# A hybrid attention and Fourier block: half of the gate products placed behind the softmax maxima, context rows spread out, and banks of its own for one product

## The chip, the cores and the metric

The kernel runs on one core of one Trainium2 chip. The metric is the device time of one execution in microseconds (us). Besides the plain runs there is one profiled execution; its trace names every instruction, its engine, its start and its length. "Span" is the time from the first to the last instruction in it. The engines are TensorE (PE in the profile, with its weight loads as PEld), VectorE (DVE), ScalarE (ACT), GpSimd (POOL) and SyncE (SP, which here only issues DMAs).

## The reference

One layer (`DEPTH = 1`) on 512 latent tokens of width 2048 and 256 context tokens, all in float32. What matters of it:

```python
shift, scale, gate = jnp.split(silu_c @ w_ada[l] + b_ada[l], 3, axis=-1)
shift_c, scale_c, gate_c = jnp.split(silu_cc @ w_ada[l] + b_ada[l], 3, axis=-1)
h = _modulate(_rmsnorm(xs, norm_g[l]), shift[:, None], scale[:, None])
hc = _modulate(_rmsnorm(cs, norm_g[l]), shift_c, scale_c)
pc_kv = hc @ w_l[:, OFF_K:OFF_ZA]              # keys and values of the context
p = h @ w_l                                    # 9216 columns: q, k, v, z_a, u_b, z_b, g_a, g_b
attn = _attention(q, jnp.concatenate([k, kc], axis=1), jnp.concatenate([v, vc], axis=1))
# _merge:
y_a = (attn * jax.nn.silu(z_a)) @ w_pa
y_b = (_fourier_mix(u_b) * jax.nn.silu(z_b)) @ w_pb
y = (g_a * y_a + g_b * y_b) @ w_o              # g_a, g_b are sigmoids of columns of p
new_xs = xs + gate[:, None] * y
return _rmsnorm(new_xs, final_g)
```

There are 12 query heads of 128 on 4 key heads; each query sees 768 keys. The vector `gate` (2048 values) is needed only at the very end, as a factor of `y`.

## The kernel before, in words

**Matrix products.** Every float32 operand is split into a high and a low part (`split_from`: ACT writes the high part, line 175, DVE subtracts it for the low part, line 176), and each product is three matmuls (`mm3`, lines 324 to 326). Large products are done as a seven-product scheme of the Strassen-Winograd kind: a `Group` works through seven products named P1, Q5, P2, Q6, P7, Q3 and Q4 on half-sized operands, and DVE combines their sums. One product has four weight pieces of 128 x 1024; a piece is 12 matmuls.

**Stages.** First a start stage (norms, modulation, the Fourier branch). Then eight projection groups `g = 0..7`: three of kind "qz" (queries and z_a), two "gate" (3 and 4, for g_a), one "kv" (5, which also works on the context), two more "gate" (6 and 7, for g_b). Then the attention: 12 heads of four query tiles are `NSTEP = 48` steps. In step i TensorE makes the scores, DVE their maximum (line 1262), ACT the exponentials (line 1264), the step before is transposed and split, and every second step the values are multiplied; `fill` puts pieces of the Fourier branch's projection (`filler`, its result taken over by DVE in line 1229) between them. Last come two branch groups (10 and 11, the attention's projection) and two output groups (8 and 9). In a branch group the seven products come in the order P1, P2, Q5, P7, Q6, Q3, Q4, in fixed banks of PSUM: "a" at bank 0, "c" at 2, "b" at 4.

**Weight stream.** `todo` lists every piece to be loaded in the order of use; `load_more` asks for pieces (SP's queue, line 211) as long as raw buffers are free and fewer than eight pieces are ahead. There are four raw buffers in `wp`; `raw0` and `raw1` in `rp` and two in `gvp` are in the list `raw_pools` for some of the time. A stage-0 product's pieces go to four buffers R instead, to which further weights are added by accumulating DMAs from POOL's queue (line 279) or by DVE (line 258); P7's pieces are differences from them (line 264).

**Gate vector.** `gate` is worked out by DVE: 32 pieces of `w_gate`, each multiplied with half a row of silu(c) (`crow[0]` for pieces 0 to 15, `crow[1]` for 16 to 31) and summed along it, in one instruction with an accumulator (`use_gate`, line 1098). `GATE_AT` says after which piece of which product in the groups the first 26 are done; the other six are asked for in attention steps 5, 10, ..., 30 and used three steps later. `load_row` brings half a row to `raw0`'s place; `silu_of_row` (lines 1088 and 1089) turns it with a tanh on ACT and a product on DVE. For the second half that is called at group 6's Q5, with a tile of `gvp` as its scratch; `gvp` lies where `qr` lay.

**Context rows.** The 256 context tokens' normalized, modulated forms are made in groups 3 and 4. `context_norm` (lines 1044 to 1047) and `context_spread` make the row of inverse norms; they stand in the list `jobs`, from which one entry is taken after each weight piece (`None` entries only count). `context_piece` says behind which piece four row blocks are worked on by `context_row` (lines 1062 to 1076), which builds seven forms in the shared buffer `qr` and stores them to `cf_d`; the kv group loads them back. `qr` is also the buffer in which rotated queries and keys are stored from (`qz_d`, `k_d`).

**Order.** The program's order is not the engines' order: the framework orders each engine's instructions by a plan of its own, with the program's order as rank. `tc.issue_after(x)` puts instructions behind x on x's engine. `use_gate` uses it with the last split.

Of the kernel before, what the change touches and what calls it, by code (L numbers as in the profile page):

```python
# [25 lines left out]
NKV = 4  # L26
# [46 lines left out]
def context_piece(g, name, pc):  # L73

    n = 28 * (g - NQZ) + 4 * ONE_GROUP.index(name) + pc
    if n % 2 == 0 and 0 <= n < 8:
        return "cn", n // 2
    if n % 6 == 0 and 18 <= n < 42:
        return "cr", n // 6 - 3

# [3 lines left out]
           + [(5, "P1", 1), (5, "Q5", 1), (5, "P2", 1), (5, "Q6", 1), (5, "P7", 1), (5, "P7", 3), (5, "Q3", 1),  # L84
              (5, "Q3", 3), (5, "Q4", 0)] + [(6, n, 1) for n in ("P2", "Q6", "P7", "Q3", "Q4")]
           + [(7, n, 1) for n in ("P1", "Q5", "P2", "Q6", "P7")])
GATE_AT = {p: q for q, p in enumerate(GATE_AT)}
NGATE = len(GATE_AT)

CHUNKS = (0, 2, 1, 3)  # L90
# [28 lines left out]
def block_kernel(ctx, tc, xT, ctx_rows, ctx_toks, x, c_row, w_ss, w_gate, vecs, qkg, rope, dft_c, dft_s,  # L119
# [178 lines left out]
    def get_aside(key):  # L298

        while not any(e.key == key for e in ahead):  # L300
            assert start_load(), key
        e = next(e for e in ahead if e.key == key)
        ahead.remove(e)
        return e.raws[0][1]

# [120 lines left out]
    for i in range(2):  # L426
        stream(("b", i), flat(b_d[i]), 1024, 2, dst=lambda: tiles("b"))
    for n, j in enumerate(CHUNKS):
        for pc in BRANCH_B:
            stream(("pab", j, pc), w_pab[j, pc], 1024, 2)  # L430
        if n + 1 < NKV:
            stream_keys(n + 1)

# [362 lines left out]
    class Group:  # L796
# [16 lines left out]
        def steps(self, name):  # L813

            form, which = next((f, c) for n, f, _, c in PRODUCTS if n == name)
            start = which not in self.acc
            if start:
# [8 lines left out]
            for pc in range(self.pieces):  # L826
# [20 lines left out]
                if q is not None:  # L847
                    use_gate(q, get(("gate", q)))
            sub = lambda o, x, y: nc.vector.tensor_tensor(o, x, y, op=ALU.subtract)
# [10 lines left out]
            elif name == "Q6":  # L860
# [3 lines left out]
                if self.g >= BRANCH_A:  # L864
                    sub(self.V, self.V, self.acc["c"])
                    self.done(1, 1, self.V, self.V)
            elif name == "P7" and self.g >= BRANCH_A:
# [5 lines left out]
            elif name == "P7":  # L873
                sub(self.V, self.V, a)
                self.done(1, 1, self.V, self.V)
            elif name == "Q3":
                if not self.last:
                    sub(self.X, a, self.X)
                self.done(0, 1, a if self.last else self.X, self.X)
            elif name == "Q4" and self.g == BRANCH_A + 1:  # L880
                self.done(1, 0, a, self.Y)
            elif name == "Q4":
                for t in ((0,), (1,)) if (self.g, name, 3) in APART else ((0, 1),):
                    t = slice(t[0], t[-1] + 1)
                    sub(self.Y[:, t, :], a[:, t, :], self.Y[:, t, :])
                self.done(1, 0, self.Y, self.Y)
# [203 lines left out]

    def ask_gate(q):
        todo.insert(0, Piece(("gate", q), [w_gate[q]], 1024, 1, "raw"))
        todo[0].aside = True

    def use_gate(q, w):

        with tc.issue_after(last_split[-1][1].ins):
            nc.vector.scalar_tensor_tensor(w, w, 0.5, crow[q // KK], op0=ALU.mult, op1=ALU.mult,
# [31 lines left out]
    for g, kind in enumerate(KINDS):  # L1130
        if g == 3:
            jobs += [lambda: None] * 10 + [context_norm, lambda: None, lambda: None, context_spread]
        elif g == KV:
# [10 lines left out]
        for name in ONE_GROUP:  # L1144
# [3 lines left out]
            elif (g, name) == (1, "Q5"):  # L1148
                silu_of_row(0, flat(new_ev()))
            elif (g, name) == (KV + 1, "Q5"):  # L1150
                silu_of_row(1, gvp.tile([P, 1024], F32, tag="raw", bufs=2, name=uid("e")))
# [15 lines left out]
            elif (g, name) == (KV + 1, "Q6"):  # L1167
                raw_pools += [(rp, 1, "raw1", 1), (gvp, 2, "raw", 2)]
            elif (g, name) == (LAST, "P7"):
# [78 lines left out]
    bheld = {}  # L1248
    NSTEP = 4 * NH

    def scores(i):
# [9 lines left out]
        mx = stats[:, 4 * (i % 4) : 4 * (i % 4) + 4]  # L1261
        nc.vector.tensor_reduce(mx[:, 0:1], sc[:, :NKEY], axis=AX.X, op=ALU.max, negate=True)
        probs[i] = take((NKEY,))
# [149 lines left out]
    for i in range(NSTEP + 3):  # L1413
# [367 lines left out]
```

## Time and profile before

| | |
|---|---|
| runs | 1345.84, 1342.2 and 1351.04 us; median 1345.84 |
| profiled execution | 1343.44 us, its span 1341.6 us |
| TensorE busy | 1290.6 us, 96% of the span, mean granted clock 0.992 |
| DVE busy | 995.6 us, 74% |
| ACT busy | 682.2 us, 51% |
| POOL busy | 180.6 us, 13% |
| DMA | 318.54 MB, mean 237 GB/s |

How to read it: "x" behind a time is a count. A group of instructions is named by line, engine, operation and tile (out<-in, without buffer numbers). In the timeline a bracket at the end of a row holds how long the engine sat idle before that instruction and what ended the wait. A table of waits has the engine and line that waited, what for, the total in us, the times and the longest. In a table of stretches the clock column is the granted TensorE clock, 1.00 being full. Some matmul records can be missing from a trace.

### The profile page before, as it was taken

Reading aid. Unit: us, or ns where it says so; the run is one execution under the profiler, and the core shown is the slowest. Engines: PE = TensorE matmul, PEld = TensorE weight load, DVE = VectorE, ACT = ScalarE, POOL = GpSimd, SP = SyncE. Lnnn points to the kernel's source line nnn. Section 1 sums busy time; section 2 is a strip of 40 time slices with the busy share of each in tenths; the row PEclk is TensorE's granted clock in tenths of the full one; section 3 lists DMA queues with packets and bytes.
Section 4 is the critical chain, followed back from the end, with each engine's and each line's share of the span. In section 5 each row is a group of like instructions: output and inputs, shape, how many; then the busy total and the mean of one; then the engine's idle time right before and its main releaser. Section 6 shows DMA issues by size and latency. Waiting matters only on the chain.

```text
span 1341.6 us, 17565 instructions
## 1 busy us (share of the span) xinstructions
PE 1290.6 (96%) x6522; PEld 1052.7 (78%) x6522; DVE 995.6 (74%) x1295; ACT 682.2 (51%) x1079; POOL 180.6 (13%) x244
## 2 busy tenths in 40 slices
PE   6999999999998989999998999899999999999997
PEld 3677888888887878887886878788888778778885
DVE  5666899889777868648676847687778767788676
ACT  5222655546455444443344534566577545465544
POOL 0110011111101001011021011112100212121210
PEclk9999999999999999999998999999999999999999
DMA  9898588888887979777877888767840889898985
GB/s 384 340 374 309 203 219 223 241 227 246 223 311 193 317 229 272 262 203 188 280 201 225 315 226 259 263 194 221 219 153 19 217 250 229 232 201 223 219 214 172
DMA packets 103718, 318.54 MB, mean 237 GB/s; under 512 B 9808, under 2 KB 33104, under 8 KB 99280
## 3 DMA queue, kind: packets, MB, share of 16 engines
q0 software_dynamic: 30288, 123.75, 39.2%
q1 hardware_dynamic: 48720, 163.65, 34.1%
q10 hardware_dynamic: 24624, 30.02, 6.4%
q8 instruction: 51, 0.84, 0.2%
q14 instruction: 35, 0.29, 0.1%
HBM read 283.30 MB, written 34.09 MB: 237 GB/s over the span
## 4 chain that ended last, share of the span: by engine, by line
PE 75%; DMA 10%; DVE 8%; ACT 3%; issue 2%; POOL 0%; SPq 0%; ACTq 0%; DVEq 0%; POOLq 0%
PE banks L324 10%; PE banks L325 10%; PE banks L326 10%; PE x L325 6%; PE x L326 6%; PE x L324 6%; PE y L325 5%; PE y L324 5%; PE y L326 5%; DVE wlo L176 3%; PE banks L1280 2%; PE pd L523 2%; DMA wr<-in_w_g 2%; PE pb L324 2%; DMA R<-in_w_g 2%
## 5 line engine op out<-in xcount | busy, mean ns | idle before, releaser
L175 ACT ACTIVATE whi<-R 128x1024 fp32r<-128x1024 f32 x138 | 145.0, 1057 | 143.1 <-PE banks L326 57.7
L176 DVE TENSOR_TENSOR wlo<-R,whi 128x1024 fp32r<-128x1024 f32 x138 | 167.5, 1220 | 51.8 <-ACT whi L175 51.2
L175 ACT ACTIVATE whi<-wr 128x1024 fp32r<-128x1024 f32 (+1 forms) x123 | 128.6, 1050 | 128.9 <-PE banks L326 35.0
L176 DVE TENSOR_TENSOR wlo<-wr,whi 128x1024 fp32r<-128x1024 f32 (+1 forms) x123 | 148.4, 1211 | 60.4 <-ACT whi L175 60.2
L324 PE MATMUL banks<-whi,s 128*128 128x512 f32 x396 | 156.7, 396 | 8.9 <-DVE R L1229 3.4
L325 PE MATMUL banks<-wlo,s 128*128 128x512 f32 x396 | 155.2, 392 | 2.0 <-DVE wlo L176 2.0
L326 PE MATMUL banks<-whi,s 128*128 128x512 f32 x396 | 155.2, 392 | 0.0
L325 PE MATMUL x<-wlo,s 128*128 128x512 f32 x352 | 138.0, 392 | 6.6 <-DVE wlo L176 6.6
L324 PE MATMUL x<-whi,s 128*128 128x512 f32 x352 | 137.7, 391 | 0.0
L326 PE MATMUL x<-whi,s 128*128 128x512 f32 x352 | 137.7, 391 | 0.0
L324 PE MATMUL y<-whi,s 128*128 128x512 f32 x316 | 123.4, 391 | 0.8 <-DVE cxe L999 0.8
L325 PE MATMUL y<-wlo,s 128*128 128x512 f32 x316 | 123.3, 390 | 0.0
L326 PE MATMUL y<-whi,s 128*128 128x512 f32 x316 | 123.0, 390 | 0.0
L279 POOL DMA_DIRECT2D R<-in_w_g x64 | 55.9, 874 | 451.5 <-DVE wlo L176 246.4
L175 ACT ACTIVATE s<-wr 128x512 fp32r<-128x512 f32 (+2 forms) x93 | 59.9, 675 | 73.9 <-DMA wr<-in_w_g 21.3
L324 PEld LDWEIGHTS banks<-whi,s 128*128 128x128 f32 x396 | 74.4, 188 | 25.4 <-ACT whi L175 6.0
L176 DVE TENSOR_TENSOR s<-wr,s 128x512 fp32r<-128x512 f32 (+2 forms) x93 | 66.5, 747 | 30.8 <-ACT s L175 30.5
L325 PEld LDWEIGHTS banks<-wlo,s 128*128 128x128 f32 x396 | 74.4, 188 | 16.8 <-DVE wlo L176 2.8
L326 PEld LDWEIGHTS banks<-whi,s 128*128 128x128 f32 x396 | 74.4, 188 | 15.5
L325 PEld LDWEIGHTS x<-wlo,s 128*128 128x128 f32 x352 | 66.4, 189 | 21.2 <-DVE wlo L176 7.5
L324 PEld LDWEIGHTS x<-whi,s 128*128 128x128 f32 x352 | 66.5, 189 | 13.8
L326 PEld LDWEIGHTS x<-whi,s 128*128 128x128 f32 x352 | 66.5, 189 | 13.8
(292 smaller groups left out, 2840.5 us busy)
## 6 DMA issues: line engine op xcount, KB each, us to landing
wr<-in_w_g SPq DMA_DIRECT2D x128, 512.0 KB, 5.2
R<-in_w_g POOLq DMA_DIRECT2D x64, 512.0 KB, 7.1
wa<-in_w_ss POOLq DMA_DIRECT2D x26, 1024.0 KB, 8.1
R<-in_w_g SPq DMA_DIRECT2D x32, 512.0 KB, 6.1
wr<-in_w_gate SPq DMA_DIRECT2D x32, 512.0 KB, 5.3
wr<-in_w_o SPq DMA_DIRECT2D x24, 512.0 KB, 6.8
R<-in_w_o POOLq DMA_DIRECT2D x24, 512.0 KB, 8.0
wr<-in_w_pab SPq DMA_DIRECT2D x20, 512.0 KB, 5.8
```

The source lines that it names most:

```text
L175: first = nc.scalar.activation(hi, src, ACT.Copy)
L176: return first, nc.vector.tensor_tensor(lo, src, hi.bitcast(F32), op=ALU.subtract)
L279: nc.gpsimd.dma_start(chain[e.pc], e.nxt, accum_op=ALU.add)
L324: nc.tensor.matmul(o, ah, bh, start=start, stop=False, skip_group_check=cont)
L325: nc.tensor.matmul(o, ah, bl, start=False, stop=False, skip_group_check=cont)
L326: nc.tensor.matmul(o, al, bh, start=False, stop=stop, skip_group_check=cont)
L523: last = nc.tensor.matmul(acc[32 * j : 32 * j + 32, :256], c2[:, 8 * h + k, :], w[:, k, :], start=n < 4, stop=n >= KK - 4)
L1280: nc.tensor.transpose(tp[:, k * P : (k + 1) * P], p[:, k * P : (k + 1) * P], ident)
```

## The change

It moves work and changes banks; no matmul is added or taken out.

- The four context row blocks go from every sixth weight piece (18, 24, 30, 36, counted from the start of group 3) to every eighth (18, 26, 34, 42). `context_norm` and `context_spread` come two entries later in `jobs`.
- `GATE_AT` keeps the 16 gate pieces of the first half (its last one moves by one weight piece). The second 16 are all used in the attention, at steps 6, 8, 11, 13, ..., 41, 43, and are now part of the stream, between the weights of the filler and the keys. They are issued behind the maximum of their step (`maxima[0]`), not behind the last split. After such a piece is taken, `load_more` is called.
- `silu_of_row(1)` is called at group 6's Q3 instead of Q5, and the two raw buffers of `gvp` join the list at group 6's Q4 instead of Q6.
- In the branch groups Q3 gets banks "d", which are those of "a", and starts a sum of its own there; it was added on top of Q6's sum in "b". DVE keeps Q6's difference in V and adds Q3's sum to it.
- The weight sums that POOL's queue prepares in the attention start at step 10 instead of 8.

```diff
-    if n % 6 == 0 and 18 <= n < 42:
-        return "cr", n // 6 - 3
+    if n % 8 == 2 and 18 <= n < 50:
+        return "cr", n // 8 - 2
...
-              (5, "Q3", 3), (5, "Q4", 0)] + [(6, n, 1) for n in ("P2", "Q6", "P7", "Q3", "Q4")]
-           + [(7, n, 1) for n in ("P1", "Q5", "P2", "Q6", "P7")])
+              (5, "Q3", 3), (5, "Q4", 1)])
...
+GATE_STEPS = [n // 2 + 6 for n in range(0, 78, 5)]
...
         ahead.remove(e)
+        load_more()
         return e.raws[0][1]
...
+    q = NGATE
     for n, j in enumerate(CHUNKS):
         for pc in BRANCH_B:
             stream(("pab", j, pc), w_pab[j, pc], 1024, 2)
-        if n + 1 < NKV:
-            stream_keys(n + 1)
+        for keys in (False, True):
+            while q < 2 * KK and (GATE_STEPS[q - NGATE] < 12 * n + 9 or keys and n + 1 == NKV):
+                stream(("gate", q), w_gate[q], 1024, 1, "raw")
+                todo[-1].aside = True
+                q += 1
+            if not keys and n + 1 < NKV:
+                stream_keys(n + 1)
...
+            if name == "Q3" and self.g >= BRANCH_A:
+                which = "d"
...
-                    use_gate(q, get(("gate", q)))
+                    use_gate(q, get(("gate", q)), last_split[-1][1])
...
                 if self.g >= BRANCH_A:
-                    sub(self.V, self.V, self.acc["c"])
-                    self.done(1, 1, self.V, self.V)
+                    sub(self.X, self.V, self.acc["c"])
+                    self.done(1, 1, self.X, self.X)
...
+            elif name == "Q3" and self.g >= BRANCH_A:
+                nc.vector.tensor_tensor(self.V, self.V, a, op=ALU.add)
+                self.done(0, 1, self.V, self.V)
...
-    def use_gate(q, w):
-
-        with tc.issue_after(last_split[-1][1].ins):
+    def use_gate(q, w, line):
+
+        with tc.issue_after(line.ins):
...
-            jobs += [lambda: None] * 10 + [context_norm, lambda: None, lambda: None, context_spread]
+            jobs += [lambda: None] * 12 + [context_norm, lambda: None, lambda: None, context_spread]
...
-            elif (g, name) == (KV + 1, "Q5"):
+            elif (g, name) == (KV + 1, "Q3"):
                 silu_of_row(1, gvp.tile([P, 1024], F32, tag="raw", bufs=2, name=uid("e")))
...
             elif (g, name) == (KV + 1, "Q6"):
-                raw_pools += [(rp, 1, "raw1", 1), (gvp, 2, "raw", 2)]
+                raw_pools.append((rp, 1, "raw1", 1))
+            elif (g, name) == (KV + 1, "Q4"):
+                raw_pools.append((gvp, 2, "raw", 2))
...
-        nc.vector.tensor_reduce(mx[:, 0:1], sc[:, :NKEY], axis=AX.X, op=ALU.max, negate=True)
+        maxima[0] = nc.vector.tensor_reduce(mx[:, 0:1], sc[:, :NKEY], axis=AX.X, op=ALU.max, negate=True)
...
-        return Group(BRANCH_A + n, bf, lambda: take((2, 512)), lambda *a: branch_done(n, *a), {"a": 0, "b": 4, "c": 2}, pieces=3)
+        return Group(BRANCH_A + n, bf, lambda: take((2, 512)), lambda *a: branch_done(n, *a), {"a": 0, "b": 4, "c": 2, "d": 0}, pieces=3)
...
-        if 8 <= i < 26:
-            n, step = divmod(i - 8, 3)
+        if 10 <= i < 28:
+            n, step = divmod(i - 10, 3)
...
-        if 5 <= i < 35 and i % 5 in (0, 3):
-            n, last = NGATE + (i - 5) // 5, i % 5 == 3
-            if not last:
-                ask_gate(n)
-            else:
-                use_gate(n, get_aside(("gate", n)))
-                if n == 2 * KK - 1:
-                    raw_pools.append((rp, 1, "raw0", 1))
+        if i in GATE_STEPS:
+            n = NGATE + GATE_STEPS.index(i)
+            use_gate(n, get_aside(("gate", n)), maxima[0])
+            if n == 2 * KK - 1:
+                raw_pools.append((rp, 1, "raw0", 1))
```

More of the change, by code (lines that the diff above doesn't have):

```diff
@@ L77, in context_piece @@
         return "cn", n // 2
-    if n % 6 == 0 and 18 <= n < 42:
-        return "cr", n // 6 - 3
+    if n % 8 == 2 and 18 <= n < 50:
+        return "cr", n // 8 - 2
 GATE_AT = ([(g, n, 1) for g in (1, 2) for n in ("P2", "Q6", "Q3")] + [(3, "Q5", 1)]
            + [(5, "P1", 1), (5, "Q5", 1), (5, "P2", 1), (5, "Q6", 1), (5, "P7", 1), (5, "P7", 3), (5, "Q3", 1),
-              (5, "Q3", 3), (5, "Q4", 0)] + [(6, n, 1) for n in ("P2", "Q6", "P7", "Q3", "Q4")]
-           + [(7, n, 1) for n in ("P1", "Q5", "P2", "Q6", "P7")])
+              (5, "Q3", 3), (5, "Q4", 1)])
 GATE_AT = {p: q for q, p in enumerate(GATE_AT)}
 NGATE = len(GATE_AT)
+GATE_STEPS = [n // 2 + 6 for n in range(0, 78, 5)]
+assert len(GATE_STEPS) == 2 * KK - NGATE
 CHUNKS = (0, 2, 1, 3)
@@ L1089, in silu_of_row @@
         nc.vector.scalar_tensor_tensor(row, e, 1.0, row, op0=ALU.add, op1=ALU.mult)
-    def ask_gate(q):
-        todo.insert(0, Piece(("gate", q), [w_gate[q]], 1024, 1, "raw"))
-        todo[0].aside = True
-    def use_gate(q, w):
-        with tc.issue_after(last_split[-1][1].ins):
+    def use_gate(q, w, line):
+        with tc.issue_after(line.ins):
             nc.vector.scalar_tensor_tensor(w, w, 0.5, crow[q // KK], op0=ALU.mult, op1=ALU.mult,
@@ L1249, in block_kernel @@
     NSTEP = 4 * NH
+    maxima = [None]
     def scores(i):
```

## The prediction

> **What bounds the kernel now.** I read the page's first part, then the busy time in stretches of 20 us, then what TensorE waited for, and last the instructions around each stretch in which TensorE fell short.
>
> ```profile
> span 1341.6 us, 17565 instructions
> PE 1290.6 (96%) x6522; PEld 1052.7 (78%) x6522; DVE 995.6 (74%) x1295; ACT 682.2 (51%) x1079; POOL 180.6 (13%) x244
> ```
>
> TensorE is the bound, busy for 1290.6 of 1341.6 us. A change that removes no matmul can give back what TensorE stands idle, and what it loses to a low clock after that, and no more. Where that is:
>
> ```profile
> 400.00:420.00 20.00, 20.00 (x90) 16.57 (x89) 17.67 (x22) 12.56 (x31) 6.99 (x7) 1.00 0.88 200
> 420.00:440.00 20.00, 16.54 (x73) 13.12 (x72) 15.20 (x19) 8.50 (x10) 3.46 (x4) 1.00 0.68 198
> 480.00:500.00 20.00, 17.97 (x80) 14.55 (x78) 13.74 (x23) 9.28 (x14) 2.57 (x3) 1.00 0.81 230
> 500.00:520.00 20.00, 17.64 (x71) 14.43 (x72) 15.61 (x26) 9.71 (x15) 1.73 (x2) 0.91 0.87 287
> 700.00:720.00 20.00, 14.98 (x53) 11.56 (x52) 10.30 (x14) 7.45 (x12) 0.12 (x1) 0.83 0.71 224
> 780.00:800.00 20.00, 16.85 (x67) 13.46 (x66) 11.65 (x13) 7.31 (x10) 1.69 (x2) 0.91 0.73 218
> 840.00:860.00 20.00, 15.09 (x68) 12.19 (x67) 11.22 (x16) 9.50 (x14) 1.96 (x3) 0.91 0.90 327
> ```
>
> The columns are stretch, length, busy time (and count) of PE, weight loads, DVE, ACT and POOL, granted clock, DMA share, GB/s. An undisturbed stretch of the projections holds 90 matmuls (400 to 420), 0.222 us each. Counting short of 90 gives what each stretch lost, clock included: 17 at 420, so **3.8 us**; 10 and 19 from 480 to 520, so **6.4**; 37 at 700, so **8.2**; 23 at 780, so **5.1**. The stretch at 840 holds other shapes; it is priced below. TensorE waited there for:
>
> ```profile
> PE x L325 <- DVE wlo L176: 6.6, 2, 3.5
> PE y L325 <- DVE s L176: 4.4, 1, 4.4
> PE x L324 <- ACT s L175: 4.2, 1, 4.2
> PE banks L324 <- DVE R L1229: 3.4, 1, 3.4
> PE banks L324 <- DVE s L849: 2.8, 2, 1.4
> PE banks L324 <- DVE ptl L176: 1.3, 1, 1.3
> ```
>
> All are waits for a split or an eviction by DVE or ACT. Both average well below full load, so the question is what those engines stood behind. In order of time:
>
> ```profile
> 398.43 0.15 DVE L1044 TENSOR_TENSOR small<-small 128x2 f32<-128x2 f32 x1
> 424.80 0.28 DVE L1047 TENSOR_SCALAR qr<-ident,small 128x128 f32<-128x128 f32 x1 [6.95 <-DMA qz_d<-qr]
> 476.25 0.48 DVE L1062 SCALAR_TENSOR_TENSOR qr<-wr,gain,qr 128x256 f32<-128x256 f32 x1 [5.74 <-DMA cf_d<-qr]
> 501.22 0.48 DVE L1062 SCALAR_TENSOR_TENSOR qr<-wr,gain,qr 128x256 f32<-128x256 f32 x1 [7.48 <-DMA cf_d<-qr]
> 708.98 1.06 ACT L1088 ACTIVATE e<-crow 128x1024 f32<-128x1024 f32 x1 [8.96 <-DMA k_d<-qr]
> 786.54 1.23 DVE L264 TENSOR_TENSOR wr<-R,wr 128x1024 f32<-128x1024 f32 x1 [11.12 <-DMA R<-in_w_g]
> 850.75 1.23 DVE L1098 SCALAR_TENSOR_TENSOR wr<-wr,crow 128x1024 f32<-128x1024 f32 x1 [4.79 <-DMA wr<-in_w_gate]
> 851.91 0.95 DVE L1262 TENSOR_REDUCE gain<-banks 128x1 f32<-128x768 f32 x1
> 944.42 1.23 DVE L1098 SCALAR_TENSOR_TENSOR wr<-wr,crow 128x1024 f32<-128x1024 f32 x1 [1.76 <-DMA wr<-in_w_gate]
> ```
>
> Every gap has the same form: an instruction that nobody needs yet stands at the head of DVE or ACT, waits there for a DMA, and the splits that TensorE needs stand behind it. The rows also show that the program's order isn't the engine's order. The gate product written for attention step 8 runs at 850.75, ahead of the first maximum (851.91). L1044 begins the job context_norm, which the program calls after the third weight piece (of four) of group 3's second product, and runs at 398.43; that product's first matmul is here:
>
> ```profile
> 408.82 0.39 PE L324 MATMUL y<-whi,s 128*128 128x512 f32 x1
> ```
>
> Its third piece ends 36 matmuls later, at about 417. What is not pinned goes forward until its data are there, in the plan's reckoning of time, and the plan reckons some DMAs shorter than they are.
>
> **The change, part by part.** The sum is made against the profiled execution, 1343.44 us (span 1341.6); the median of the three runs is 2.4 us above it.
>
> *Context rows from 6 to 8 pieces apart.* The rows share one buffer, qr, and each row must wait until its predecessor's cf_d store has read it.
>
> ```profile
> 484.11 0.33 SPq L211 DMA_DIRECT2D wr<-in_ctx_rows  x1
> 490.76 0.33 ACTq L1076 DMA_DIRECT2D cf_d<-qr  x1
> ```
>
> The store issued at 490.76 releases the last row's first instruction at 501.22, and DVE stands for 7.48 us. The last row moves from piece 36 to 42 after the start of group 3. Among those six pieces four (P2's) need a raw buffer, so its load, now at 484.11, comes behind four weight loads, after about 500; the row can't stand at DVE's head before its load. Nothing then waits at 494 to 501: **-6.4 us**. The third row moves by four pieces, two of them with a load; it may still meet the wait at 476.25, which stops no matmul now (460 to 480 has no entry in TensorE's waits). Bounds: 0 if another row stands there, 6.4 if none. I take 6.4. The later last store holds the ACT queue's table load behind it some microseconds later than now; ACT stood there without cost before, I take 0 against at most the 6.4 that this place has shown.
>
> *context_norm two jobs later.* L1047 waits 6.95 us for qr. Two pieces are 5.4 us, so if the job were pinned, the wait would shrink to 1.5 and the 3.8 us would go. But the job isn't pinned; L1044 ran some 18 us ahead of its place. Bounds 0 and 3.8; the nearest row is L1044's, so **0**.
>
> *Tanh of the second half-row at Q3 instead of Q5 of group 6.* Its target lies where qr lay, and it stands at ACT's head until the k_d store has landed, 8.96 us.
>
> ```profile
> 709.95 1.14 ACT L175 ACTIVATE s<-wr 128x512 fp32r<-128x512 f32 x2
> 715.36 0.33 SPq L211 DMA_DIRECT2D wr<-in_w_gate  x1
> ```
>
> The split of P2's fourth piece (709.95) is the one TensorE waited for. With the tanh four products later in the program, the splits of P2 and Q6 rank ahead of it, and its buffer is free by 709 in any case. Also, no gate load takes a raw buffer here any more (such as the one at 715.36), so P2's fourth load goes one place earlier. If the tanh is moved forward again, it meets the same 8.96 us: bounds 0 and 8.2. I take **-8.2**, since several splits that are ready now outrank it. The two extra raw buffers come three products later; groups 3 and 4 run at 90 matmuls per stretch with no more buffers than remain, so 0.
>
> *Ten gate products out of groups 6 and 7 and into the attention, each behind its step's maximum.*
>
> ```profile
> L1098 DVE SCALAR_TENSOR_TENSOR wr<-wr,crow x32: 1205/1217/1226, 272.4 to 948.2; 128x1024 f32<-128x1024 f32 x32
> L1098 DVE DVE_READ_ACCUMULATOR wr<-wr,crow x32: 77/82/85, 273.5 to 949.3; 128x1 f32 x32
> wr<-in_w_gate SPq DMA_DIRECT2D x32, 512.0 KB, 5.3
> 843.17 0.33 SPq L211 DMA_DIRECT2D wr<-in_w_gate  x1
> 854.00:858.00 4.00, 4.00 (x19) 3.38 (x18) 1.25 (x4) 2.04 (x5) 0.55 (x1) 0.57 0.71 206
> 880.00:900.00 20.00, 20.00 (x140) 18.08 (x139) 17.36 (x29) 14.82 (x30) 3.32 (x6) 1.00 0.73 251
> 1020.00:1040.00 20.00, 20.00 (x142) 18.41 (x141) 18.91 (x30) 15.35 (x31) 0.87 (x1) 1.00 0.09 24
> ```
>
> One costs DVE 1.22 + 0.08 = 1.30 us; ten are 13 us, and ten loads of 0.5 MB go with them on SP's queue. In the attention, 880 to 900 holds two of them with TensorE at 20.00 of 20, and 1020 to 1040 has DVE at 18.91 of 20, TensorE still full. So 1.30 us every 2.5 steps (about 10 us) is hidden by the next transposes and filler matmuls. If that cover were gone, all ten cost 13. I charge one, **+1.3**, because the last (step 43) stands just ahead of the full stretch at 1020.
>
> What they give: a gate pinned behind its maximum can't stand ahead of step 0. The wait of 4.79 at 850.75 goes, and with it TensorE's 3.44 us idle and the 4 us at a clock of 0.57 behind it, 4 x 0.43 = 1.7: **-5.2**. The pair at 944 goes too, with the 1.29 on ptl: **-1.3**. This holds only if the loads are early. Following the program's requests through the five raw buffers, today's first gate finds no free buffer when it is asked for (843.17, landing 850.7); in the new order every gate is asked for at least two steps before its use, about 8 us against a median 5.3 to landing.
>
> The Trainium skill (TensorE: Matmul & The Clock Gate, the clock table) says that the clock halves after an idle window of about 3.4 us that runs freely; 854 to 858 at 0.57 agrees, while 420 to 440 at 1.00 after 3.46 us idle shows the free phase. By that rule alone, the idle at 850 would be worth 3.4 or 5.1; my sum uses the row.
>
> *Sixth product's own banks.* In the branch groups Q3 gets banks that P1 and P2 have left, so it needn't wait until DVE has read Q6's sum: L849, twice 1.4. The DVE work is the same count, three subtractions, then one addition for one subtraction. But behind the second place TensorE waits again:
>
> ```profile
> 1166.12 0.50 PE L325 MATMUL banks<-wlo,s 128*128 128x512 f32 x1 [1.28 <-DVE wlo L176]
> ```
>
> That split hangs on a weight load, not on TensorE, so coming 1.4 us earlier there only lengthens this wait. Bounds 1.4 and 2.8; I take **-1.4**.
>
> *The rest.* The weight sums two steps later keep their DMAs and are needed only after the attention; the last gate of the first half one piece later delays the row's load by some 4 us, before an ACT that is 40 us away: 0. The 5.1 at 780 (L264 behind R's accumulating DMA) isn't touched on purpose. Two gates less ahead of it and less DMA traffic could shorten it; bounds 0 and 5.1, the wait of 11.12 is far longer than 2 x 1.30, so **0**.
>
> Sum: -6.4 - 8.2 - 5.2 - 1.3 - 1.4 + 1.3 = -21.2; 1343.4 - 21.2 = **1322 us**.
>
> **Rivals.**
> *The plan goes by readiness, not by place.* The moved tanh and rows go forward again and meet the same stores. Only what is pinned or structural stays: -5.2 - 1.3 - 1.4 + 1.3 = -6.6, so 1337 us. For it: L1044's 18 us. Against: the last row's later load.
> *Everything goes.* L1047's 3.8, the 5.1 at 780 and the second 1.4 go as well, and the 1.3 is hidden: 1322.2 - 3.8 - 5.1 - 1.4 - 1.3 = 1311 us.
> *Slower: pinned gates whose loads are late.* A gate now stands right behind the maximum, ahead of the splits of the probabilities and the filler's eviction, and can't be put off. Each late load then costs what 850.75 cost, 5.2 us. With n late ones among sixteen: 1322 + 5.2 n (the two of today are already taken out); from n = 5 on it is slower than 1343.4, and with eight it is 1364. For it: five raw buffers shared with keys, values and filler weights, and loads of gates have been late twice among six. Against: the requests are earlier. The Trainium skill (TensorE: Matmul & The Clock Gate, the table of specifications) calls VectorE's queue strictly first in, first out; the row at 850.75, with the maximum behind it, agrees, and that rule is what makes this rival dear.
>
> **How the numbers follow.** Forecast 0.56, readiness 0.17, everything 0.14, late loads 0.13. What a measurement can tell apart from no change is about 1% (13 us); the three runs lie 9 us apart. The forecast's own spread is a term of 6 to 8 us up or down, so 0.51 of its 0.56 falls beyond 1%; with "everything" that is 0.65 faster. Readiness (-0.5%) and the rest of the forecast with two or three late loads make 0.24 the same, and late loads from five on 0.11 slower. The range goes from 1309, under "everything", to 1343, which takes in readiness and up to four late loads.
>
> **What would show it.** Right: no waits of DVE on cf_d near 500 and of ACT on k_d near 709, 90 matmuls in every stretch there; gates in the attention at distances of about 10 us, none with a wait on in_w_gate; no wait on L849 in the branch groups. Wrong: L1062 or L1088 again behind their stores; gates waiting for loads with a clock below 0.7 after them; a new wait on raw buffers in group 6; TensorE idle in the attention behind ptl or L1229 with no DMA involved.

## The result

The changed kernel takes 1327.74 us (median; 1325.23 to 1329.0), beside 1346.37 us for the kernel before in runs taken with it. The ratio is 0.9858, with an interval of 0.9822 to 0.9895: 1.4% faster, and 6 us above the 1322 that was forecast. Some 3 of these 6 are the base: the forecast was counted from 1343.44, and the kernel before came out at 1346.37. The gain is 18.6 us for 21.2 forecast. The profiled execution took 1329.0 us, with a span of 1327.0.

All lines of the file have moved. The conversions of the split, 175 and 176, are now 176 and 177; the diagonal product of `context_norm` is 1060, `context_row` 1075, the tanh 1101, the gate product 1107, the difference behind R 265, DVE's take-over of sums 859, the matmuls of a product 326 to 328, the exponentials 1276, the transposes of the attention 1292 and of the branch groups 1406 (before 1394).

The page's first lines, then the busy time in stretches (columns as before):

```profile
span 1327.0 us, 17532 instructions
PE 1290.2 (97%) x6522; PEld 1053.7 (79%) x6522; DVE 994.9 (75%) x1295; ACT 683.9 (52%) x1079; POOL 180.8 (14%) x244
...
420.00:440.00 20.00, 16.41 (x60) 12.94 (x59) 13.77 (x17) 8.51 (x12) 3.13 (x4) 0.83 0.68 193
480.00:500.00 20.00, 20.00 (x90) 16.57 (x89) 19.47 (x30) 9.98 (x16) 3.46 (x4) 1.00 0.65 168
500.00:520.00 20.00, 20.00 (x90) 16.57 (x89) 10.79 (x20) 9.70 (x14) 0.00 (x0) 1.00 0.93 313
520.00:540.00 20.00, 19.13 (x84) 15.48 (x84) 17.56 (x20) 8.49 (x11) 3.45 (x4) 1.00 0.94 246
540.00:560.00 20.00, 18.80 (x84) 15.12 (x83) 12.73 (x13) 11.29 (x13) 0.00 (x0) 1.00 0.92 312
700.00:720.00 20.00, 16.81 (x62) 12.97 (x61) 9.37 (x11) 8.29 (x11) 0.86 (x1) 0.83 0.62 199
780.00:800.00 20.00, 20.00 (x90) 16.57 (x89) 10.87 (x13) 9.45 (x14) 3.47 (x4) 1.00 0.92 240
900.00:920.00 20.00, 16.29 (x96) 14.18 (x96) 12.30 (x21) 10.31 (x20) 3.94 (x6) 0.83 0.81 232
```

TensorE's busy time is what it was (1290.2 after 1290.6), so all that came off is idle time. Counted against 90 matmuls as before: 480 to 520 is full (it lost 6.4 us), 780 is full (it lost 5.1). But 420 is 30 short, 6.7 us after 3.8; 700 is 28 short, 6.2 after 8.2; 520 to 560, which held 90 and 90 before, is 12 short, **2.7 us lost anew**; and 900, which held 135, holds 96.

Three rows of each trace cut the span into parts: the first matmul behind the projections, and the first and last transposes of the branch groups. First the kernel before, then after:

```profile
844.98 0.47 PE L324 MATMUL banks<-whi,s 128*128 128x512 f32 x1 [1.47 <-DVE ev L849]
1082.65 1.03 PE L1394 MATMUL banks<-ident,s 128*128 128x128 f32 x8
1188.61 1.03 PE L1394 MATMUL banks<-ident,s 128*128 128x128 f32 x8
```

```profile
837.85 0.47 PE L326 MATMUL banks<-whi,s 128*128 128x512 f32 x1 [1.47 <-DVE ev L859]
1072.91 1.04 PE L1406 MATMUL banks<-ident,s 128*128 128x128 f32 x8
1173.95 1.04 PE L1406 MATMUL banks<-ident,s 128*128 128x128 f32 x8
```

The projections are 7.1 us shorter (forecast 14.6), the attention 2.6 (237.67 to 235.06; forecast 5.2), the branch groups 4.9 (105.96 to 101.04; forecast 1.4), and the rest is equal (152.99 and 153.05). That is 14.6 us of span in all. This profiled execution is the longest of the four, and that of the kernel before was 2.9 us below its median, so this sum is smaller than the difference of the medians (18.6).

What stood at the head of DVE and ACT in the places that still lose time, and in those that no longer do:

```profile
426.02 0.28 DVE L1060 TENSOR_SCALAR qr<-ident,small 128x128 f32<-128x128 f32 x1 [6.82 <-DMA qz_d<-qr]
509.44 0.88 DVE L1075 SCALAR_TENSOR_TENSOR qr<-wr,gain,qr 128x256 f32<-128x256 f32 x2 [6.08 <-DMA cf_d<-qr]
524.73 1.29 DVE L934 SCALAR_TENSOR_TENSOR qr<-qr 128x512 f32<-128x512 f32 x2 [1.31 <-DMA qr<-in_qkg]
543.51 1.15 ACT L176 ACTIVATE s<-wr 128x512 fp32r<-128x512 f32 x2 [4.47 <-DMA wr<-cf_d]
709.27 1.06 ACT L1101 ACTIVATE e<-crow 128x1024 f32<-128x1024 f32 x1 [9.72 <-DMA k_d<-qr]
769.32 1.22 DVE L265 TENSOR_TENSOR wr<-R,wr 128x1024 f32<-128x1024 f32 x1 [1.88 <-DMA R<-in_w_g]
```

The last context row still waits 6.08 us behind its store, but no matmul needs DVE just then (480 to 520 is full). What follows it is late instead: the rotation table (L934) stands ahead of a low part at 525, and the conversion at 543 waits for the last `cf_d` to be read back. The diagonal product and the tanh are where they were, to 1.3 us, though the program calls the one two jobs and the other four products later. In place of the one wait of 11.12 us on R at 786 there are three short ones, the longest 1.88. No gate product in the attention waits for its load any more. One weight of the filler does:

```profile
893.76 0.33 SPq L212 DMA_DIRECT2D wr<-in_w_pab  x1
901.97 1.06 ACT L176 ACTIVATE whi<-wr 128x1024 fp32r<-128x1024 f32 x1 [3.62 <-DMA wr<-in_w_pab]
906.29 0.69 PE L1292 MATMUL banks<-ident,s 128*128 128x128 f32 x2 [3.70 <-ACT s L1276]
```

Its load went out at 893.76, when the gate product at 892.50 gave its raw buffer back. ACT stood before its conversion; the low part on DVE waited for that conversion, the next maxima stood behind the low part, the exponentials waited for the maxima, and TensorE was idle for 3.70 us.

### The profile page after: what moved, and what is told of

It reads as the page before. It is cut to its first block, busy times and chain, and to the rows that moved or that the text cites. A ratio compares the mean times of both kernels' runs of the same rounds, so it can differ in the third digit from the quotient of the medians.

```text
span 1327.0 us, 17532 instructions
## 1 busy us (share of the span) xinstructions
PE 1290.2 (97%) x6522; PEld 1053.7 (79%) x6522; DVE 994.9 (75%) x1295; ACT 683.9 (52%) x1079; POOL 180.8 (14%) x244
## 4 chain that ended last, share of the span: by engine, by line
PE 69%; DMA 15%; DVE 9%; ACT 4%; issue 3%; POOL 0%; ACTq 0%; SPq 0%; DVEq 0%; POOLq 0%
PE banks L326 9%; PE banks L327 9%; PE banks L328 9%; PE x L327 6%; PE x L328 6%; PE x L326 6%; PE y L327 4%; PE y L326 4%; PE y L328 4%; DMA s<-in_w_pab 3%; DVE wlo L177 3%; DMA wr<-in_w_g 2%; PE pd L531 2%; DMA cf_d<-qr 2%; DVE s L177 2%
```

## The experiments

Each ratio is to the kernel before, run beside it on the same chip, with its 95% interval; 0.002 is 2.7 us. A profile shows one execution, and in six of the twelve experiments it was the shortest of its runs, so it serves to find the place, and the ratio to price it.

**Banks alone.** Kernel before, with the sixth product's own banks.

```diff
+            if name == "Q3" and self.g >= BRANCH_A:
+                which = "d"
...
-                    sub(self.V, self.V, self.acc["c"])
+                    sub(self.X, self.V, self.acc["c"])
```

> The kernel before with only the sixth product's own banks. Theory: the two waits on L849 (1.4 us each) go and the wait that the prediction saw behind them (1.28 at 1166) goes too, since the changed kernel's branch stage was 6.9 us shorter: 1346 - 5 to 7, about 1340 us. Rival (the prediction's own reading): the wait behind the second place takes that gain back, 1.4 us in all, 1345 us.

1340.14 us, 0.9958 (0.9935 to 0.9982), as the theory had it. The branch groups took 101.5 us in its profile; in all eleven profiles with these banks it is 100.9 to 102.2, in the three without them 106.0 to 106.7. So the banks are worth **4.9 us**, not 1.4. Where the part beyond the two waits on Q6's sum comes from shows on DVE, first in the kernel before, then in the changed kernel (the kernel with the banks alone has the same order):

```profile
1161.45 1.21 DVE L849 TENSOR_TENSOR s<-s,banks 128x1024 f32<-128x1024 f32 x1
...
1163.72 1.22 DVE L1378 TENSOR_TENSOR s<-s,s 128x1024 f32<-128x1024 f32 x1
1164.85 2.35 DVE L176 TENSOR_TENSOR wlo<-R,whi 128x1024 fp32r<-128x1024 f32 x2
```

```profile
1146.85 1.21 DVE L859 TENSOR_TENSOR s<-s,banks 128x1024 f32<-128x1024 f32 x1
...
1149.11 1.22 DVE L1390 TENSOR_TENSOR s<-s,s 128x1024 f32<-128x1024 f32 x1
1150.48 2.36 DVE L177 TENSOR_TENSOR wlo<-R,whi 128x1024 fp32r<-128x1024 f32 x2 [0.15 <-ACT whi L176]
```

The wait of 1.28 us at 1166 was not for a weight load, as I had said: the low part stood behind three DVE operations (the middle one is left out here). These came late because another low part, at 1160.31, stood ahead of them and waited 1.98 us for ACT. Now the three follow Q6's sum at once, and the low part is there in time. Why the plan orders them otherwise now isn't shown. The two waits of 1.41 and the one of 1.28, 4.1 of the 4.9 us, are gone.

**Rows alone.** Kernel before, with the rows and the norm at their new places.

```diff
-    if n % 6 == 0 and 18 <= n < 42:
+    if n % 8 == 2 and 18 <= n < 50:
...
-[lambda: None] * 10 +
+[lambda: None] * 12 +
```

> The kernel before with only the context rows eight pieces apart and the norm job two entries later. Theory: the wait of DVE for cf_d at 501 goes (6.3 us), two new short waits of TensorE in group 4's last two products take 2.7 back, the wait for qz_d near 424 stays: 3.6 us less, about 1342.5 us; with the clock dip at 427 that the changed kernel shows, 1345. Rival: the short waits came from other parts of the change, so 6.3 us less, 1340 us.

1347.18 us, 1.0005 (0.9986 to 1.0024): nothing, where the theory had 3.6 us (about 1 with the clock dip) and the rival 6.3; both missed. The stretches from 480 to 560 in its profile:

```profile
480.00:500.00 20.00, 20.00 (x90) 16.57 (x89) 19.61 (x31) 9.89 (x15) 3.43 (x4) 1.00 0.63 167
500.00:520.00 20.00, 20.00 (x90) 16.55 (x89) 10.46 (x19) 9.76 (x14) 0.00 (x0) 1.00 0.93 309
520.00:540.00 20.00, 19.22 (x85) 15.57 (x84) 16.85 (x19) 8.28 (x12) 3.45 (x4) 1.00 0.94 240
540.00:560.00 20.00, 18.48 (x82) 14.87 (x81) 13.16 (x15) 11.04 (x14) 0.00 (x0) 1.00 0.93 304
```

The 6.4 us at 480 to 520 did go, and 2.9 us come back at 520 to 560, with the waits of L934 and of the `cf_d` load that the changed kernel shows too. In this profile the place at 420 also lost more than before (30 matmuls short, 6.7 us against 3.8).

**Gates alone.** The change without the banks, the rows and the norm's place.

```diff
+GATE_STEPS = [n // 2 + 6 for n in range(0, 78, 5)]
...
-            elif (g, name) == (KV + 1, "Q5"):
+            elif (g, name) == (KV + 1, "Q3"):
...
-                    use_gate(q, get(("gate", q)))
+                    use_gate(q, get(("gate", q)), last_split[-1][1])
```

> The kernel before with only the gates' part: sixteen gate products in the attention behind the maxima, tanh at Q3, raw buffers later, weight sums later; rows and banks as before. Theory: groups 6 and 7 give 7 us (5.1 at 782, 2.0 at 710 with the tanh still behind the store), the attention almost nothing, because a late filler weight takes back there what the gates' waits cost: about 1339 us. Rival: the attention gives its 6.5 us and the late weight was the other parts' doing: about 1333 us.

1331.93 us, 0.9877 (0.9834 to 0.9919): most of the gain, and the rival's time. The place at 780 is full in its profile, at 700 it is 22 short. Its attention is 230.56 us long, the shortest of all fourteen traces: the late weight of the filler is hardly there (TensorE idle for 1.36 us at 900, after 3.70 in the changed kernel). That was the rival's reason too: the rows or the banks, which this kernel lacks, would then bring that weight late. One execution shows it, and how isn't shown.

**Six gates.** The change, but ten gate products left in groups 6 and 7, the tanh at Q5 and the buffers at Q6 as before; only the six of the attention are behind the maxima.

```diff
-              (5, "Q3", 3), (5, "Q4", 1)])
+              (5, "Q3", 3), (5, "Q4", 1)] + [(6, n, 1) for n in ("P2", "Q6", "P7", "Q3", "Q4")]
+           + [(7, n, 1) for n in ("P1", "Q5", "P2", "Q6", "P7")])
...
-GATE_STEPS = [n // 2 + 6 for n in range(0, 78, 5)]
+GATE_STEPS = [8, 13, 18, 23, 28, 33]
```

> The changed kernel with ten gate products left in groups 6 and 7 as before (tanh at Q5, raw buffers at Q6), so that only six are in the attention, at steps 8, 13, ..., 33, streamed and behind their maxima. Theory: the gates in groups 6 and 7 are what made DVE stand at 786, so 5 us of the gain go there, and with fewer gates in the raw buffers no filler weight is late in the attention, which gives 5 us: both together the changed kernel's 1328 within 2 us. Rival one: the wait at 786 was a matter of the plan's order and does not come back: 1323 us. Rival two: the late weight stays: 1333 us.

1340.0 us, 0.9953 (0.9928 to 0.9979); theory and rivals had it at 1333 or less, so all three missed. The wait at 780 is back (the row stands with the next kernel). Beside the banks alone (0.9958) there is next to nothing, although its profile has the attention 4.1 us shorter.

**Early buffers.** As six gates, but with all sixteen in the attention: the two kernels differ in the place of the gate products only (ten move out of groups 6 and 7, and the six of the attention come at later steps).

```diff
-            elif (g, name) == (KV + 1, "Q3"):
+            elif (g, name) == (KV + 1, "Q5"):
...
-                raw_pools.append((rp, 1, "raw1", 1))
-            elif (g, name) == (KV + 1, "Q4"):
-                raw_pools.append((gvp, 2, "raw", 2))
+                raw_pools += [(rp, 1, "raw1", 1), (gvp, 2, "raw", 2)]
```

> The changed kernel with the sigmoid's tanh at the product Q5 of group 6 and two buffers given over at Q6, both as before the change; the ten gate products stay behind the maxima in the attention, the rows and the banks stay as changed. Theory (the ten gate weights' loads and products in groups 6 and 7 took the buffers and so made the loads of R late at 780 us): 780 to 800 us stays free of stalls, the stall at 698 to 717 us is back to 7 to 8 us instead of 5.0, and the time is 1328 to 1332. Rival (it is the buffers given over later, or the tanh, that freed 780 us): the product near 780 loses 5 to 7 us again, the attention starts at 842 to 846 us and the time is 1333 to 1337.

1330.2 us, 0.9879 (0.9852 to 0.9906). The stretch at 780 in this kernel, then in six gates:

```profile
780.00:800.00 20.00, 20.00 (x90) 16.55 (x89) 10.01 (x11) 9.22 (x11) 2.59 (x3) 1.00 0.87 222
```

```profile
780.00:800.00 20.00, 15.85 (x60) 12.56 (x59) 11.68 (x13) 8.14 (x11) 1.75 (x2) 0.83 0.72 204
```

So it was the ten gates in groups 6 and 7 that made R late, and not the tanh or the buffers: the theory. Their move is worth **0.0074, 10 us** (uncertain by 5), the largest part of the change: 6.7 us is this place, the rest isn't placed. In the four profiles with the ten in groups 6 and 7 (before, banks alone, rows alone, six gates) this stretch is 23 to 30 matmuls short; in the ten with them moved it is full. The same two sets differ in the four accumulating DMAs that bring R just before: they land after 8.4 to 14.8 us with the ten gates there, and after 5.3 to 8.6 without. In the kernel before, SP's queue issues two gate loads at 762 and weight loads from 765 on, and 2.94 MB of such loads move beside these DMAs (764 to 787); in the changed kernel the weight loads begin at 752, and 1.03 MB move beside them (760 to 779). That points at the loads more than at DVE's products, though no run parts the two. The place at 700, for which the theory had 7 to 8 us, is full here as well, for a reason that shows below (a store of 4.9 us). From this kernel to the changed one (0.9858 and, again, 0.9862) the tanh and the buffers bring about 2 us, which the intervals don't tell from nothing.

**Tanh held.** The change, with the tanh put behind the conversion that the program had just issued.

```diff
+        with tc.issue_after(last_split[-1][0].ins) if half else nullcontext():
             nc.scalar.activation(e, row, ACT.Tanh, scale=0.5)
```

> The changed kernel with the second half-row's tanh pinned on ACT behind the last split that the program has issued there. Theory: at 710 the tanh stands before the last half of P2's fourth split and waits for the k_d store; pinned, the 6 us of that stretch (28 matmuls short of 90) go: 1328 - 6 = 1322 us. Rival: the split itself would have been late (its weight load), and half of it stays: 1325 us.

1324.1 us, 0.9849 (0.9818 to 0.9881). The tanh runs at 726.75 without a wait, and 700 to 720 is full although the store still took 16.8 us; in the changed kernel it is 28 short:

```profile
700.00:720.00 20.00, 20.00 (x90) 16.58 (x89) 14.73 (x16) 10.43 (x13) 3.43 (x4) 1.00 0.93 258
```

**Norm held.** The change, with the diagonal products behind a conversion of group 3's third product.

```diff
-        for b in range(2):
-            nc.vector.tensor_scalar(diag[:, b, :], ident, ss[:, b : b + 1], None, op0=ALU.mult)
+        with tc.issue_after(behind[0].ins):
+            for b in range(2):
+                nc.vector.tensor_scalar(diag[:, b, :], ident, ss[:, b : b + 1], None, op0=ALU.mult)
```

> The changed kernel with the norm's two diagonal products pinned on DVE behind the last split of group 3's third product. Theory: the 6.82 us wait for the qz_d store then lies behind the splits that TensorE needs, the stretch from 420 to 440 loses nothing, 6.7 us less with the clock dip: 1321 us. Rival: the rows start later and meet their stores in group 4 again, which takes 3 to 6 us back: 1325 to 1328 us.

1324.62 us, 0.9859 (0.9827 to 0.9891). The place at 420 is empty of idle time:

```profile
420.00:440.00 20.00, 20.00 (x90) 16.57 (x89) 14.49 (x17) 10.45 (x12) 3.48 (x4) 1.00 0.87 247
```

**Sixth buffer.** The change, with one more raw buffer in the attention.

```diff
+    spare = free.pop()
+    raw_pools.append((spare[0], 1, spare[1], 1))
```

> The changed kernel with a sixth raw buffer during the attention (a free slot), until the last gate product. Theory: the filler weight whose load was issued at 893.8, when a gate released its buffer, loads earlier; ACT does not stand 3.6 us for it and TensorE not 3.7 us behind that, with the clock dip 5 us less: 1323 us. Rival: the split is planned ahead of its load in any case and another one is late: 1328 us.

1326.69 us, 0.9863 (0.9837 to 0.9888). The filler's load went out earlier, and 900 to 920 is full:

```profile
883.88 9.15 SPq L212 DMA_DIRECT2D wr<-in_w_pab  x2
...
900.00:920.00 20.00, 20.00 (x139) 17.56 (x138) 16.04 (x28) 13.89 (x29) 3.19 (x6) 1.00 0.86 283
```

Each of the three mends clears its place in the profile, and none of them alone is told from the changed kernel by its ratio. With four runs each, a difference to the changed kernel is uncertain by some 5 us, so a part of the 5 to 7 us expected of each could hide here.

**All three.** The tanh held, the norm held and the sixth buffer together.

> The changed kernel with all three: tanh pinned, diagonal products pinned, sixth raw buffer. Theory: the three gains lie in different stages and add up: 1328 - 6 - 6.7 - 5 = about 1310 us. Rival: a new order of the plan brings waits of its own, as it did at 906: 1315 to 1320 us.

1317.86 us, 0.9807 (0.9776 to 0.9837): the rival's time, 1315 to 1320, and not the sum of the three (1310). The attention is 232.55 us long. The three places together:

```profile
420.00:440.00 20.00, 19.93 (x89) 16.17 (x88) 15.62 (x20) 10.88 (x14) 3.47 (x4) 1.00 0.89 253
...
700.00:720.00 20.00, 20.00 (x90) 16.57 (x89) 16.52 (x18) 9.27 (x13) 3.45 (x4) 1.00 0.90 248
900.00:920.00 20.00, 19.56 (x131) 16.68 (x128) 17.21 (x30) 14.53 (x27) 3.54 (x6) 1.00 0.81 248
```

**The changed kernel again**, on the chip of the next two.

> The changed kernel itself once more, on the chip on which the next three run, so that they can be set against it. Theory (its stages: third products of group 3 lose 6.8, group 5's products 1.2 and 1.5, group 7's third product 5.0, the wait on a late filler weight in the attention about 4): the ratio 0.986 as before, 1324 to 1329 us, with the same three places of idle time. Rival (two executions of one program differ by where transfers fall, as the store of 5.9 against 16.5 us in the kernel with the banks alone did): one of the three places empty in this execution and the time 4 to 7 us under the others.

1327.32 us, 0.9862 (0.9837 to 0.9886). One place is empty in this execution, as the rival said, but the time isn't lower, so neither is right as written: 700 to 720 is full, while 420 is 33 short, 520 is 27 short, and 900 holds 85. The store of the keys, in the first trace of this kernel and in this one:

```profile
k_d<-qr ACTq DMA_DIRECT2D x2, 256.0 KB, 16.6
```

```profile
k_d<-qr ACTq DMA_DIRECT2D x2, 256.0 KB, 5.2
...
700.00:720.00 20.00, 20.00 (x90) 16.53 (x89) 16.58 (x19) 11.36 (x15) 3.31 (x4) 1.00 1.00 282
```

The same program, and the store lands after 16.6 us or after 5.2. Over all fourteen traces it is 4.9 to 5.2 in three and 15.8 to 17.0 in eleven, with nothing between. The tanh was not held in any of the three; in these its wait is at most 1.61 us, and the place at 700 loses 0.9 us at most.

**Rows six apart, with the mends.** All three mends, with rows and norm at their old places (the diagonal products stay held).

```diff
-    if n % 8 == 2 and 18 <= n < 50:
+    if n % 6 == 0 and 18 <= n < 42:
```

> The kernel with all three mends (tanh held behind a conversion, diagonal products held behind a conversion, a sixth raw buffer), with the context rows 6 jobs apart and the norm at the tenth job, as before the change. Theory: the four stores of cf_d and their readers come back to 486 to 500 us, the product that starts near 490 loses 4 to 6 us again and the ones near 521 and 533 lose nothing: 2 to 4 us slower than with the rows 8 apart (1317.9 there), 1319 to 1322. Rival (rows apart are worth nothing, since the rotation table and the last cf_d load take back all of it, as in the kernel with the rows alone): 1317 to 1319, with 1 to 2 us lost at 490 and as much more gained at 521 to 540. Second rival (rows 6 apart need the diagonal products where they were, and with these held back the first row waits): 1322 to 1326.

1317.11 us, 0.9791 (0.9768 to 0.9814). The time is the first rival's: the rows are worth nothing. The places are the theory's: 480 to 520 loses 4.4 us again (16 and 4 short), and 520 to 560 nothing, where the kernel with all mends lost 4.7 from 500 to 560.

```profile
480.00:500.00 20.00, 17.20 (x74) 13.85 (x73) 12.06 (x23) 9.55 (x14) 3.43 (x4) 0.97 0.90 256
500.00:520.00 20.00, 20.00 (x86) 16.42 (x85) 15.92 (x24) 10.46 (x16) 1.72 (x2) 0.95 0.90 278
520.00:540.00 20.00, 20.00 (x90) 16.57 (x89) 14.71 (x17) 8.99 (x12) 1.73 (x2) 1.00 0.96 283
```

**Table held.** All three mends, with the rotation table's products behind a conversion.

```diff
-                rotations(1.0)
+                with tc.issue_after(last_split[-1][1].ins):
+                    rotations(1.0)
```

> The kernel with all three mends, and the two products of the rotation table in group 5 held behind the conversion that the program has just issued. Theory (in the kernel with the mends the products near 521 and 533 lose 1.75 and 1.73 us; the first is the table, 1.3 us of VectorE after a wait of 1.3 us for its load, ahead of a weight's low part): 500 to 520 us and 520 to 540 us hold 85 to 90 matmuls instead of 84 and 82, and the time is 1 to 2 us lower, 1316 to 1317. Rival (the wait is the weights' own load, since the loads after the stores of cf_d come late whatever VectorE does): the same matmuls and 1318, within 1 us of the kernel with the mends.

1317.96 us, 0.9796 (0.9774 to 0.9819): the rival's time, but only half its reason. TensorE's wait of 1.44 us behind the table, at 522, is gone. The next ones, at 540 and 542, are 2.9 us together instead of 1.43, behind conversions that wait for loads, and the clock drops after them, so 540 to 560 holds 66 matmuls instead of 83:

```profile
529.25 1.06 ACT L176 ACTIVATE whi<-wr 128x1024 fp32r<-128x1024 f32 x1 [4.35 <-DMA wr<-in_w_g]
538.14 1.15 ACT L176 ACTIVATE s<-wr 128x512 fp32r<-128x512 f32 x2 [3.92 <-DMA wr<-cf_d]
```

The three kernels with all mends are the fastest here and can't be told apart. On the chip of the last two, the changed kernel had 1327.32, so the mends bring 9.4 and 10.2 us together. Why each alone shows so little isn't settled. On that chip eleven runs of the last two kernels lie within 1316.65 to 1320.12, six of the changed kernel within 1323.97 to 1329.88, eleven of the kernel before within 1339.18 to 1351.51; the four runs of the kernel with all three mends, on another chip, lie within 1316.14 to 1323.3, so the narrow spread isn't sure either. It would fit waits that come and go with the landing of transfers, one showing where another is removed, but no run isolates it.

## Why the prediction was right or wrong

The time was 1327.7 for a forecast of 1322, inside its range, on the right side. Step by step it was less good, and that the total came near is in good part luck: of the 14.6 us forecast for rows and tanh some 2 came, while the place that was put at 0 brought up to 10 and the banks 3.5 more than forecast.

- **Rows, -6.4: wrong.** The wait behind the store did stop costing TensorE, as said, but alone and with the mends the move is worth 0 (1.0005; 0.9791 beside 0.9807 and 0.9796). The failed step is "The later last store holds the ACT queue's table load ... I take 0": the table, the weights' loads and the reading back of the last `cf_d` took the gain with the mends (4.7 us lost there for 4.4 saved). Alone they took 2.9 of the 6.4, and the place at 420 lost 2.9 more than before. I named the right successor and priced it at nothing because the old trace had slack there. The row itself also waits still (6.08): its later load didn't keep it from standing at DVE's head before its store.
- **Tanh, -8.2: wrong; the rival by readiness was right here.** The tanh, called four products later, ran at 709.27 instead of 708.98. "Several splits that are ready now outrank it" is the failed step: the plan put the tanh ahead of them. That it reckons the store shorter than the 16 us it takes would explain this, but no run shows what it reckons. I had the evidence in L1044's place and used it for the norm alone. About 2 us came (0.9879 to 0.9862), from the tanh or the buffers, not told from nothing.
- **Norm, 0: the cause right, the size off in this trace.** The diagonal product went forward again, to 426.02. The prediction put its place a product too early: the eleventh entry comes behind the third piece of group 3's third product, not its second, so L1044 had gone forward by some 11 us more than I said. The place lost 2.9 us more than before; that is the clock, below.
- **Gates in the attention, -5.2 in all: right in the waits, and then half taken back.** The waits at 850 and 944 are gone and no gate is late. The attention is 2.6 us shorter, and 5.1 with all mends (232.55 us). What stands out in this trace is the filler's late weight at 902, with TensorE idle for 3.70 us: the slower rival's mechanism, a late load at the head of an engine, with n = 1 and a weight in the gate's place. With a sixth buffer it is gone from its place, but that attention is still 234.10 us long, so this weight isn't all of the difference; the rest isn't placed.
- **780, 0: wrong.** "Isn't touched on purpose" was no reason. Ten loads and products fewer ahead of R are worth 10 us by ratio, 5.1 of them in this place in the changed kernel's profile. In the place the upper bound came, and I took the lower: I named the lighter DMA traffic and then weighed the wait (11.12) only against DVE's 2 x 1.30. The DMAs that bring R landed up to 14.8 us after their issue with the ten gates and at most 8.6 without, so the loads are the likelier cause; a run with the loads alone moved was not tried.
- **Banks, -1.4: mis-sized, 4.9.** The reason for taking back the second 1.4 ("that split hangs on a weight load") was not read from DVE's rows; it hung on three DVE operations that the change moves forward.

By ratio the change splits into four steps from kernel to kernel: banks 5.7 us, six gates with the rows and the later weight sums 1, ten gates 10, tanh and buffers 2. They add up to the whole because each starts where the one before ended, so the sum is no check of them; the first is uncertain by some 3 us, the others by some 5. Of the signs named, the waits behind the stores of `cf_d` and `k_d` stayed (wrong), with full stretches at 480 to 520 and not at 700; gates without a wait, and no wait on Q6's sum in the branch groups, came (right).

## What to carry to other kernels

An instruction that waits for a DMA at the head of an in-order engine costs what stands behind it; calling it later in the program didn't help here, where a plan orders the engine by its own reckoning, and tying it behind a neighbour cleared its place in the profile. Ask of every load that a change takes away what shares its buffers and DMA engines next, even if the edit isn't aimed there: here that was the largest gain. And before a gain is booked, price what the moved thing meets at its new place by that place's own rows.

## What the hardware showed

**A store with two durations.** The 256 KB stores of the keys land after about 5 or about 16.5 us in executions of one program (rows above). Between 688 and 712 us of the changed kernel, the DMA queues moved this:

```profile
q0 software_dynamic: 576, 2.10, 45.7%
q1 hardware_dynamic: 796, 2.87, 32.0%
q10 hardware_dynamic: 1056, 0.52, 7.5%
```

The columns are packets, MB and share of time; q10 has the stores. A packet of the stores is 0.49 KB (0.52 MB over 1056), one of the loads 3.6 KB. The Trainium skill (DMA: Bandwidth & Descriptors, Queues, rings and completion order) says that each DMA engine takes turns between its queues packet by packet; if these are the packets of the profile, small ones beside two busy queues of large ones would make a slow store, which agrees with the long case. It doesn't explain the short one, and what chooses between them stays open.

**The clock behind an idle time.** The idle time at 426, and the 4 us from 428, first in the kernel before, then after:

```profile
426.27 0.50 PE L325 MATMUL x<-wlo,s 128*128 128x512 f32 x1 [3.46 <-DVE wlo L176]
...
428.00:432.00 4.00, 4.00 (x19) 3.32 (x18) 4.00 (x5) 1.86 (x3) 0.00 (x0) 1.00 0.82 263
```

```profile
427.50 0.79 PE L327 MATMUL x<-wlo,s 128*128 128x512 f32 x1 [3.59 <-DVE wlo L177]
...
428.00:432.00 4.00, 4.00 (x11) 3.04 (x10) 4.00 (x7) 0.00 (x0) 0.00 (x0) 0.50 0.70 256
```

An idle time 0.13 us longer, and the next 4 us ran at 0.50 instead of 1.00. The Trainium skill (TensorE: Matmul & The Clock Gate, the clock table and the note below it) has the clock halve after an idle window of about 3.4 us, which runs freely. These two rows agree with it, others do not. Ten of the traces have an idle time in this place: behind 2.43, 2.44, 2.51, 3.39, 3.40, 3.59, 3.95 and 5.10 us the clock fell to about half, behind 2.66 and 3.46 it stayed at 1.00. So here an idle time of 2.4 us can already halve the clock, and the length alone doesn't say which will; past the first 10 us of the span, all 17 idle times of 3.54 us and more in the fourteen traces did. An idle time between 2.4 and 3.5 us has two prices, and nothing here shows the 3 us by which they differ at 426 to be an effect of the edit.
